# Moving the output projection behind the next block's last convolution, and the first weight loads behind the first transposes, in a two-layer hybrid encoder step

## The chip, the cores and the metric

The kernel runs on one core of one Trainium2 chip. The engines are named as in the profile: PE (TensorE matmul, with PEld for its weight loads), DVE (VectorE), ACT (ScalarE), POOL (GpSimd) and SP (SyncE, whose queue starts most DMA transfers). The metric is the device time of one execution in microseconds (us), as the median of several runs; less is better. "Span" is the time from the first to the last instruction of the profiled execution.

## The reference

One step of a streaming encoder with two layers. Layer A is a gated recurrent block; layer B is sliding-window attention over keys and values that are computed once from layer A's result. There are two groups of rows: a prompt of 4096 rows and a "sample" group of 8 x 16 = 128 rows with a saved state. The model width is 1024. Layer A, cut to what matters here:

```python
def a_layer(x, conv_hist, h0, norm_g, w_in, conv_w, conv_b, wa, ba, wx, bx, lam, w_out):
    u = rms_norm(x, norm_g) @ w_in
    xb, gate = u[..., :D_RNN], u[..., D_RNN:]
    xc, conv_new = causal_conv(xb, conv_hist, conv_w, conv_b)    # width 4
    h, h_last = rglru(xc, h0, wa, ba, wx, bx, lam)
    y = (h * jax.nn.silu(gate)) @ w_out
    return x + y, conv_new, h_last

def rglru(x, h0, wa, ba, wx, bx, lam):
    ...
    r = jax.nn.sigmoid(gr)      # gr, gi: two products of x with 256 x 256 gate blocks
    i = jax.nn.sigmoid(gi)
    log_a = RG_C * r * jax.nn.log_sigmoid(lam.astype(jnp.float32))
    a = jnp.exp(log_a)
    b = jnp.sqrt(-jnp.expm1(2.0 * log_a)) * (i * xf)
    ...
    _, h = lax.associative_scan(comb, (a, b), axis=1)
```

Layer B (queries, windowed softmax with sinks, a second gated projection) isn't touched by the change, except for three transfers that it starts early.

## The kernel before

**Precision.** Every matrix product is made of three float16 products: an operand is split into a high and a low part (`hi`, `lo`), and `mm3` (L221) issues hi x hi, hi x lo, lo x hi for each of the 8 slices of the contraction. So a product over 1024 channels is 24 matmuls. Weights are split at the start of the kernel: `Prep` (L105) loads a weight tile, takes the largest absolute value of each of its slices (`largest`, L126: L132 on ACT, L134 on DVE), gets one scale from them through a tiny PE product (`inv_scale`, L94), and `finish` (L153) writes `hi` (L172, L175) and `lo` (L173, L176) into the same tile. The activations before the output projection are split in the same way, with a scale taken from their own largest value (`BlockA.split`, L543).

**Blocks.** The prompt is 16 blocks of 256 rows. For layer A a block does four pairs p of 256 channels. `conv(p)` is 48 matmuls for the left half of `w_in`, then ACT copies the result (`U`, L462), POOL and DVE make the four taps (`xc`, L474 and L476) and `xchl` holds the split of it (L478, L479). `silu(p)` is 48 matmuls for the right half and gives `v` (L487, L488). `gates(p)` (L491) is 24 matmuls for r and i from `xchl`, then a chain on ACT (`tr`, `ti`, `th`, `a`) and DVE (`ti`, the scan L526) that gives `hg` and its largest value `amax` (L539). When all four pairs are there, `split` makes the scale (PE, then DVE `m2h` to `ish`) and then `hghl`: four `hi` on ACT (L554), four `lo` on DVE (L555). `out(u)` (L561), for u = 0 to 3, is 24 matmuls of `hghl` with `w_out` (128 rows x 512 columns), adds the input rows `xr` again (L572), stores the sum, and after the last of them `norm_out` (L581) computes the row norm and writes the rows, split, to the DRAM buffer `xq` for layer B. A block's own input comes from `load` (rows `xt`), `rstd` (squares, L415), `norm` (L418: `xp` as hi on ACT, lo on DVE, L213 and L214) and four DMA transposes into `xn` (L426).

**Order.** PE's instructions run in the order in which they are written. From the third block on (i = 2 to 15; i = 1 has its own branch) one turn of the loop in `layer_a` (L605) gives PE this: conv(0), silu(0), gates(3) of the block before, conv(1), silu(1), gates(0), conv(2), silu(2) with the scale of the block before in its middle, gates(1), the four out(u) of the block before, conv(3), silu(3), gates(2). In the last turn (i = 15) one out(u) stands there, and the other three later. The other engines' queues are ordered when the program is built, by a simulated timeline; what each then runs is fixed. `after(e, i)` puts the instructions of a `with` body behind instruction i in the queue of i's engine. `step()` hangs pieces of layer B's weight preparation (`bw`, `bp`) between these parts.

**Start.** The sample group `bs` is loaded first, then block 0 (`b0`). The loads of the first pairs' weights go through `e.wload`, which is ACT's queue for pair 0, the first gates and pair 1, and SP's queue afterwards; nothing ties a load to the transposes, so the builder's order decides. `w0` to `w3` are the four pairs' weight tiles, `w5` and `w6` hold raw slices for them.

Of the kernel before, what the change touches and what calls it, by code (L numbers as in the profile page):

```python
# [10 lines left out]
F32 = mybir.dt.float32  # L11
# [8 lines left out]
P = 128  # L20
# [83 lines left out]
class Prep:  # L104
# [6 lines left out]
    def __init__(self, e, w, src, ranges, ends, pool, act=()):  # L111
        nc = e.nc
        self.act = act
        self.e, self.w, self.ranges, self.pool = e, w, ranges, pool
        pieces, wid = w.shape[1:]
        n_in = pieces - 2
        self.raw = [w[:, k + 2] for k in range(n_in)]
        for h in range(0, n_in, 3):
            g = min(h + 3, n_in)
            e.wload(w[:, h + 2:g + 2], src[:, h:g])  # L120
        self.src = src[:, n_in:]
        self.mx = e.sm.tile([P, len(ranges)], F32, name=f"mx{len(ranges)}", bufs=2 if len(ranges) < 8 else 3)
        self.largest(range(n_in))
        if ends is not None:
            self.rest(ends)
# [11 lines left out]
    def rest(self, ends):  # L137

        if isinstance(ends, list):
            for k, t in enumerate(ends):  # L140
                self.e.wload(t, self.src[:, k])
        else:
            self.e.wload(ends, self.src)
            ends = [ends[:, k] for k in range(2)]
        n = len(self.raw)
        self.raw += ends
        self.largest((n, n + 1))
        return self
# [115 lines left out]
def a_weights_head(e):  # L264

    nc = e.nc
    v = e.vec
    work = e.tmp.tile([P, 2, NB], F32, name="tr", bufs=1).rearrange("p a b -> p (a b)")
    t, z, z2, acc = (work[:, KT * i:KT * i + KT] for i in range(4))
    lam = v[:, V_LAM]  # L270
    nc.scalar.activation(t, lam, AF.Abs)
    nc.scalar.activation(t, t, AF.Exp, scale=-1.0)
    nc.vector.tensor_scalar(z, t, 2.0, None, op0=OP.add)
    nc.vector.reciprocal(z, z)
    nc.vector.tensor_tensor(z, z, t, op=OP.mult)
    nc.vector.tensor_tensor(z2, z, z, op=OP.mult)
    nc.vector.tensor_scalar(acc, z2, 1.0 / 21, 1.0 / 19, op0=OP.mult, op1=OP.add)
    for d in (17, 15, 13, 11, 9, 7, 5, 3, 1):
        nc.vector.tensor_tensor(acc, acc, z2, op=OP.mult)
        nc.vector.tensor_scalar(acc, acc, 1.0 / d, None, op0=OP.add)  # L280
    nc.vector.tensor_tensor(acc, acc, z, op=OP.mult)
    nc.vector.tensor_scalar(t, lam, 0.0, None, op0=OP.min)
    nc.vector.scalar_tensor_tensor(t, acc, -2.0, t, op0=OP.mult, op1=OP.add)
    e.clh = e.keep.tile([P, KT], F32, name="clh")
    e.nclh = e.keep.tile([P, KT], F32, name="nclh")
    nc.vector.tensor_scalar(e.clh, t, 4.0, None, op0=OP.mult)
    nc.vector.tensor_scalar(e.nclh, t, -4.0, None, op0=OP.mult)
# [104 lines left out]
class BlockA:  # L392
# [25 lines left out]
    def norm(self):  # L418
# [3 lines left out]
        for st, x in enumerate(self.x):  # L422
            hi, lo = self.xp[st], e.tmp.tile([P, 1024], F16, name="xp", bufs=3)
            pair_rows(e, x, self.r[:, st:st + 1], hi, lo)
            for a, t in enumerate((hi, lo)):
                nc.sync.dma_start_transpose(out=self.xn[:, a, :, st * P:(st + 1) * P], in_=t)  # L426
        self.mx = e.sm.tile([P, 4], F32, name="amax")

    def proj(self, p, half, mid=None):
# [130 lines left out]
    def out(self, u, each=False):  # L560
# [7 lines left out]
        W = e.wO[o]  # L568
        run(mm3(e, ps, lambda k, a: h[:, a, k, st * P:(st + 1) * P], lambda k, b: part(W, k, b, 0, 512), range(KT)))
        x = e.tmp.tile([P, 512], F32, name=e.t_res, bufs=e.b_res)  # L570
        e.load(x, self.src[st, :, 512 * o:512 * o + 512])
        dve = nc.vector.scalar_tensor_tensor(x, ps, self.inv[:, o:o + 1], x, op0=OP.mult, op1=OP.add)  # L572
        e.anchor = dve, e.anchor[1]
        e.store(e.x1[self.bi][st, :, 512 * o:512 * o + 512], x)
# [31 lines left out]
def layer_a(e):  # L606
# [2 lines left out]
    blocks = [BlockA(e, i) for i in range(e.nblk)]  # L609
    b0 = blocks[0]  # L610
    bs.load()
    e.wload = lambda o, i: e.nc.scalar.dma_start(o, i)
    bs.rstd()
    bs.norm()
    b0.load()
    a_weights_head(e)
    a_pair_load(e, 0)
    a_pair_gload(e, 0)
    a_pair_load(e, 1)
    e.wload = e.load  # L620
    a_pair_in(e, 0)
    b0.rstd()
    b0.norm()
    a_pair_gload(e, 1)
    a_pair_gin(e, 0)
    for p in range(4):
        bs.conv(p)
# [11 lines left out]

        b0.conv(p, mid)  # L640
        if p < 3:
            with after(e, e.prep[p + 1][0].ready):
                if p < 2:
                    a_pair_load(e, p + 2)
                    a_pair_gload(e, p + 2)
# [8 lines left out]
        bs.gates(p)  # L654
    e.store(e.outs["s_conv"], e.sconv)
    e.store(e.outs["s_h"], e.sh0)
    a_out_load(e)
    prev = b0
    wb = b_weights(e)
    for i in range(1, e.nblk):  # L660
# [51 lines left out]
        if first:  # L712
# [8 lines left out]
            b.gates(2)  # L721
            cache_load(e)
        else:
            for o in range(1 if last else 4):
                prev.out(o, last)
                step()
            b.conv(3, step)
            step()
            if last:
                e.store(e.outs["p_conv"], e.hist)  # L730
            b.silu(3)
# [136 lines left out]
def b_consts(e):  # L868
# [13 lines left out]

    qk, e.qsc, e.nsf, e.bias = k([P, 2, 64]), k([P, 18]), k([P, 8]), k([P, 192])
    e.nsink, e.nsfs, e.bias_s, e.nsink_s = k([P, 8]), k([P, 2]), k([P, 2, 144]), k([P, 2])
    e.load(store[:, 0:used[0]], e.ins["b_consts"])
    e.gk = qk[:, 1]
    f = k([P, 64])
    nc.vector.scalar_tensor_tensor(f, qk[:, 0], 0.125, qk[:, 1], op0=OP.mult, op1=OP.mult)
# [365 lines left out]


def layer_b(e, prev, tail):
    e.store(e.outs["s_old"], e.ins["cache_tail"])
    e.cc0 = e.tmp.tile([P, 2, 2, 384], F16, name="cc0", bufs=1)
    bs = BlockB(e, -1)
    bs.xn = e.xs  # L1260
# [86 lines left out]
def tile_kernel(ctx, tc, ins, outs):  # L1347
# [8 lines left out]
    e.big = pool("big", 1)  # L1356
    e.dram = pool("dram", 1, space=DRAM)
    e.load = lambda o, i: nc.sync.dma_start(o, i)
    e.wload = e.load
    e.store = lambda o, i: nc.sync.dma_start(o, i)  # L1360
    e.cols = e.keep.tile([P, 96], F32, name="cols")
    e.one8 = e.keep.tile([P, KT], F32, name="one8")
# [111 lines left out]
```

## Time and profile before

| | |
|---|---|
| median of 3 runs | 2738.92 us (2738.11 to 2741.18) |
| the profiled execution | 2738.68 us, of which its span is 2736.3 us |
| busy in the span | PE 2568.0, DVE 1941.0, ACT 1631.3, POOL 510.9 us |
| DMA | 295.80 MB in 538494 packets |
| PE's granted clock, mean | 0.976 |

The page of the profile gives busy time by engine, then 40 slices of the span with one digit per slice (tenths busy; for PEclk the granted clock in tenths). The timeline lists instructions in order of time, equal neighbours merged: start, duration, engine, line, operation, tiles, count, and in brackets the idle time before it and what ended that. The table of windows gives, for each stretch: its length, each engine's busy time (and instructions), the granted clock, the DMA share and GB/s. The table of waits gives who waited for whom: us in total, times, longest. The chain of waits follows the work that ended last back from the end.

### The profile page before, as it was taken

The numbers are of one execution on the slowest core, as the hardware profiler recorded it, in microseconds if no ns is written. First come the engines' busy times: TensorE is split into PE (matmuls) and PEld (weight loads), VectorE is DVE, ScalarE is ACT, GpSimd is POOL, SyncE is SP. The second block draws the span as 40 slices with busy tenths as digits, with TensorE's granted clock in tenths as the row PEclk, the third lists the DMA queues.
The fourth block names the chain that finished last, engine by engine and source line by source line (L and its number), as shares of the span: only waits on it lengthen the run. The fifth ranks groups of instructions, "written<-read, shape, count | busy, mean of one in ns | idle before, by whom it ended". The sixth has DMA issues, their size and how long they took to land.

```text
span 2736.3 us, 51574 instructions
## 1 busy us (share of the span) xinstructions
PE 2568.0 (94%) x18838; PEld 1773.6 (65%) x18838; DVE 1941.0 (71%) x6101; ACT 1631.3 (60%) x3784; POOL 510.9 (19%) x624
## 2 busy tenths in 40 slices
PE   3788999999999999999998999999999999999998
PEld 2675677666677766667756656666665566666654
DVE  5977776667676676767666867777777677777675
ACT  4765675565676756567645655555555555555554
POOL 1432111111111111111112211111222111112220
PEclk9889999999999999999999999999999999999999
DMA  7032333333232433333555555454544554545444
GB/s 267 9 103 71 90 77 111 101 107 110 83 109 88 147 101 108 109 89 100 197 145 155 107 114 109 109 108 95 100 91 105 112 109 110 108 96 102 90 89 97
DMA packets 538494, 295.80 MB, mean 108 GB/s; under 512 B 454384, under 2 KB 467696, under 8 KB 536688
## 3 DMA queue, kind: packets, MB, share of 16 engines
q1 hardware_dynamic: 537232, 287.80, 42.1%
q10 hardware_dynamic: 1008, 4.72, 0.4%
q8 instruction: 147, 2.41, 0.4%
q14 instruction: 107, 0.88, 0.1%
HBM read 112.05 MB, written 66.86 MB: 65 GB/s over the span
## 4 chain that ended last, share of the span: by engine, by line
PE 56%; DVE 16%; ACT 13%; DMA 6%; issue 6%; POOL 2%; SPq 0%; ACTq 0%; DVEq 0%; POOLq 0%
PE pm L229 51%; DVE xc L476 4%; PE pa L1099 3%; PE po L1144 3%; DMA xn<-xp 2%; DVE ti L526 2%; ACT a L510 1%; ACT th L509 1%; ACT ti L508 1%; DMA xq<-xp 1%; POOL xc L474 1%; ACT L513 1%; DVE hg L538 1%; ACT tr L507 1%; DVE ti L515 1%
## 5 line engine op out<-in xcount | busy, mean ns | idle before, releaser
L229 PEld LDWEIGHTS <-w 128*128 128x128 f16 x9792 | 943.5, 99 | 161.8 <-issue 26.2
L229 PE MATMUL pm<-xn,w 128*128 128x256 f16 (+1 forms) x8064 | 900.3, 273 | 44.0 <-DMA xn<-xp 29.9
L229 PE MATMUL pm<-w,hghl 128*128 128x512 f16 x3120 | 729.0, 389 | 57.3 <-ACT hghl L554 52.0
L229 PEld LDWEIGHTS <-hghl 128*128 128x128 f16 x3120 | 303.8, 100 | 430.4 <-ACT hghl L554 56.4
L1107 ACT ACTIVATE s<-s,negm 128x192 f32<-128x192 f32 (+2 forms) x512 | 226.5, 443 | 194.9 <-DVE negm L1104 193.3
L1122 DVE SCALAR_TENSOR_TENSOR ph<-s,ri,ph 128x64 f16<-128x64 f32 x1008 | 247.4, 314 | 46.0 <-ACT ph L1118 45.8
L229 PEld LDWEIGHTS <-w4b 128*128 128x128 f16 x1968 | 190.6, 99 | 114.0 <-issue 9.9
L1104 DVE CUSTOM_DVE_ANT_0 s<-pa,cst 128x192 f32<-128x192 f32 (+2 forms) x512 | 223.0, 470 | 45.0 <-PE pa L1099 42.9
L1118 ACT ACTIVATE ph<-s,ri 128x192 f16<-128x192 f32 (+2 forms) x512 | 191.0, 440 | 87.2 <-ACT d L1249 54.8
L476 DVE SCALAR_TENSOR_TENSOR xc<-U,cws,xc 128x256 f32<-128x256 f32 (+1 forms) x408 | 181.2, 477 | 18.0 <-POOL xc L474 17.8
L1156 POOL TENSOR_TENSOR hghl<-hg,hghl 128x512 f16<-128x512 f32 (+1 forms) x65 | 75.4, 1170 | 617.5 <-DVE xt L1238 523.9
L229 PE MATMUL pm<-w,xn 128*128 128x512 f16 x816 | 183.3, 381 | 5.4 <-DVE xn L555 3.5
L229 PEld LDWEIGHTS <-xn 128*128 128x128 f16 x1200 | 116.5, 98 | 103.0 <-issue 4.7
L229 PE MATMUL pm<-w4b,w 128*128 128x256 f16 x1536 | 176.9, 273 | 0.0
L229 PE MATMUL pm<-w,w4b 128*128 128x512 f16 x768 | 172.9, 381 | 0.0
L465 POOL COPY hist<-U 128x6 f32<-128x6 f32 x60 | 16.9, 281 | 633.6 <-ACT U L462 633.6
L474 POOL TENSOR_SCALAR xc<-U,cws,cbs 128x256 f32<-128x256 f32 (+1 forms) x136 | 114.7, 850 | 77.5 <-DVE ti L514 23.8
L1099 PE MATMUL pa<-kT,qT 128*128 128x192 f16 (+2 forms) x1024 | 125.1, 245 | 4.0 <-ACT qT L1061 4.0
L1099 PEld LDWEIGHTS <-qT 128*128 128x128 f16 x1024 | 91.5, 98 | 40.7 <-ACT qT L1061 5.3
L1048 POOL TENSOR_TENSOR qh<-qf,qh 128x512 f16<-128x512 f32 x66 | 77.8, 1198 | 185.4 <-ACT qh L1047 185.4
L220 ACT ACTIVATE junk<-xr 128x512 bf16<-128x512 f32 x60 | 37.5, 624 | 124.9 <-DVE xr L572 120.1
L229 PE MATMUL pg<-xchl,w4b 128*128 128x256 f16 (+1 forms) x816 | 95.8, 274 | 12.3 <-POOL w4b L176 7.1
(286 smaller groups left out, 3559.2 us busy)
## 6 DMA issues: line engine op xcount, KB each, us to landing
xt<-in_xp_dram SPq DMA_DIRECT2D x32, 512.0 KB, 4.4
xt<-x SPq DMA_DIRECT2D x64, 256.0 KB, 2.7
out_yp_dram<-xt SPq DMA_DIRECT2D x64, 256.0 KB, 2.3
xr<-in_xp_dram SPq DMA_DIRECT2D x58, 256.0 KB, 4.6
x<-xr SPq DMA_DIRECT2D x58, 256.0 KB, 2.1
xq<-xp SPq DMA_DIRECT2D x58, 256.0 KB, 3.5
bw<-in_b_q_dram SPq DMA_DIRECT2D x32, 256.0 KB, 3.4
bw<-in_b_gate_dram SPq DMA_DIRECT2D x32, 256.0 KB, 3.1
```

The source lines that it names most:

```text
L229: nc.tensor.matmul(ps, w(k, a), x(k, b), start=(i == 0 and j == 0), stop=(i == len(ks) - 1 and j == 2))
L474: nc.gpsimd.tensor_scalar(o, tap(t, 0), e.cws[:, 0, j:j + 1], e.cbs[:, 0, j:j + 1], op0=OP.mult, op1=OP.add)
L476: dve = nc.vector.scalar_tensor_tensor(o, tap(t, k), e.cws[:, k, j:j + 1], o, op0=OP.mult, op1=OP.add)
L526: nc.vector.tensor_tensor_scan(h[:, t], a[:, t], ti[:, t], 0.0 if self.sample else e.carry[:, j:j + 1], op0=OP.mult, op1=OP.add)
L1048: nc.gpsimd.tensor_tensor(qh[:, :, 1], qf, qh[:, :, 0], op=OP.subtract)
L1099: nc.tensor.matmul(ps[:, y, lo:192], qT[:, j2 + y, c], self.kT[:, 2 * g + x, k0 + lo:k0 + 192], start=x == 0, stop=x == 1)
L1104: nc.vector.tensor_tensor_reduce(s_[:, y, lo:192], ps[:, y, lo:192], e.bias[:, lo:], scale=e.nsf[:, h:h + 1], scalar=e.nsink[:, h:h + 1], ...
L1107: nc.scalar.activation(s_[:, y, lo:192], s_[:, y, lo:192], AF.Exp, bias=negm[:, j:j + 1], scale=-1.0, accum_out=den[:, j:j + 1])
L1118: nc.scalar.activation(hi[:, lo:], ss[j][:, lo:192], AF.Copy, scale=ri[:, j:j + 1])
L1122: nc.vector.scalar_tensor_tensor(ph[:, j, to:to + n], ss[j][:, cols], ri[:, j:j + 1], hi[:, cols], op0=OP.mult, op1=OP.subtract)
L1144: nc.tensor.matmul(po[64 * g:64 * g + 64, :], V[:, 64 * g:64 * g + 64], PT[g][:, :, b, :], start=i == 0, stop=i == len(prods) - 1)
L1156: nc.gpsimd.tensor_tensor(self.hl[:, 1][sl], og, hi, op=OP.subtract)
```

## The change

Two things are moved, and nothing is added to the arithmetic. First, in the loop of layer A, for i = 2 to 14 the four out(u) of the block before, and for i = 15 the one out(u), stand behind conv(3) of the running block and ahead of its silu(3). Second, the start of layer A is put in another order: all weight loads go through SP's queue; the sample group's `rstd` and `norm` get high priority for the builder; pair 0's weights are loaded ahead of block 0's rows; the gates' weights and pair 1 are put behind the sample group's transposes (`turned`, the last of them), pairs 2 and 3 behind block 0's; and the residual rows `xr`, the output weights, layer B's constants and the copy of the old cache stay behind block 0's transposes too.

```diff
-            e.wload(w[:, h + 2:g + 2], src[:, h:g])
+            e.load(w[:, h + 2:g + 2], src[:, h:g])
...
             for a, t in enumerate((hi, lo)):
-                nc.sync.dma_start_transpose(out=self.xn[:, a, :, st * P:(st + 1) * P], in_=t)
+                self.turned = nc.sync.dma_start_transpose(out=self.xn[:, a, :, st * P:(st + 1) * P], in_=t)
...
         x = e.tmp.tile([P, 512], F32, name=e.t_res, bufs=e.b_res)
-        e.load(x, self.src[st, :, 512 * o:512 * o + 512])
+        with after(e, e.turned):
+            e.load(x, self.src[st, :, 512 * o:512 * o + 512])
...
     bs.load()
-    e.wload = lambda o, i: e.nc.scalar.dma_start(o, i)
-    bs.rstd()
-    bs.norm()
...
+    with e.tc.high_priority():
+        bs.rstd()
+        bs.norm()
+    a_pair_load(e, 0)
     b0.load()
     a_weights_head(e)
-    a_pair_load(e, 0)
-    a_pair_gload(e, 0)
-    a_pair_load(e, 1)
-    e.wload = e.load
     a_pair_in(e, 0)
     b0.rstd()
     b0.norm()
-    a_pair_gload(e, 1)
+    with after(e, bs.turned):
+        a_pair_gload(e, 0)
+        a_pair_load(e, 1)
+        a_pair_gload(e, 1)
     a_pair_gin(e, 0)
...
         b0.conv(p, mid)
         if p < 3:
-            with after(e, e.prep[p + 1][0].ready):
+            with after(e, e.prep[p + 1][0].ready), after(e, b0.turned):
...
     e.store(e.outs["s_h"], e.sh0)
-    a_out_load(e)
+    e.turned = b0.turned
+    with after(e, e.turned):
+        a_out_load(e)
...
         else:
+            b.conv(3, step)
+            step()
             for o in range(1 if last else 4):
                 prev.out(o, last)
                 step()
-            b.conv(3, step)
-            step()
```

**SP's queue at the start**, from the sample group's rows `xt` on. Before (`xn<-xp` are the transposes; `w` are weight tiles; rows of the same transfers that follow each other are merged):

```order
L1358 DMA xt<-in_xs_dram 128x1024
L1358 DMA xt<-in_xp_dram 128x1024
L298 DMA sstate<-in_state_conv_dram 128x192
L301 DMA sstate<-in_state_rglru_dram 128x64
L1358 DMA w_218<-in_a_gates_dram 128x1024
L1358 DMA w_624<-in_a_w_in_dram 128x1536 x2
L1358 DMA w_219<-in_a_w_in_dram 128x1024
L1358 DMA w_218<-in_a_gates_dram 128x1024
L1358 DMA w_1022<-in_a_w_in_dram 128x1536 x2
```

Six more transfers follow there (weights, `hghl`, two of `xr`), and then the sample group's two transposes, the 19th and the 21st transfer of the queue. The same place now, from the same transfer on:

```order
L1363 DMA xt<-in_xs_dram 128x1024
L1363 DMA w_164<-in_a_w_in_dram 128x1536 x2
L1363 DMA w_136<-in_a_w_in_dram 128x1024
L1363 DMA xt<-in_xp_dram 128x1024
L296 DMA sstate<-in_state_conv_dram 128x192
L299 DMA sstate<-in_state_rglru_dram 128x64
L421 DMA_TRANSPOSE xn<-xp 128x8x128 x2
L1363 DMA xt<-in_xp_dram 128x1024
L1363 DMA w_135<-in_a_gates_dram 128x1024
L1363 DMA w_335<-in_a_w_in_dram 128x1536 x2
L1363 DMA w_136<-in_a_w_in_dram 128x1024
L1363 DMA w_135<-in_a_gates_dram 128x1024
```

Pair 0's weights (`w_164`, `w_136`) came to this queue from ACT's; the two transposes of the sample group moved ahead of pair 1 (`w_335`), which came from ACT's queue too. Block 0's four transposes stand right behind these rows, ahead of pairs 2 and 3.

**DVE at the start**, in the second half of the split of pair 0's weights (`w_220`, now `w_164`; `mx_250`, now `mx_338`, are the largest values of pair 1's weights, `w_247`, now `w_335`; `w_219`, now `w_136`, holds raw slices of both). Before:

```order
L134 TENSOR_REDUCE mx_250<-w_247 128x1 x3
L173 SCALAR_TENSOR_TENSOR w_220<-w_220,gs_262 128x512
L362 TENSOR_SCALAR sstate<-sstate,cols 128x48
L350 TENSOR_TENSOR pairw<-pairw,acw 128x2
L173 SCALAR_TENSOR_TENSOR w_220<-w_220,gs_262 128x512
L351 TENSOR_TENSOR pairw<-pairw,vabs 128x2
L134 TENSOR_REDUCE mx_250<-w_219 128x1 x2
L173 SCALAR_TENSOR_TENSOR w_220<-w_220,gs_262 128x512
```

Three more low parts (L173) follow there, and block 0's row norm behind them. Now, as far as the last low part and the reductions of pair 1's gates (`mx_350`):

```order
L134 TENSOR_REDUCE mx_338<-w_335 128x1 x3
L173 SCALAR_TENSOR_TENSOR w_164<-w_164,gs_239 128x512
L205 TENSOR_TENSOR rtn_301<-ryn_300 128x2
L173 SCALAR_TENSOR_TENSOR w_164<-w_136,gs_239,w_164 128x512
L134 TENSOR_REDUCE mx_338<-w_335 128x1 x3
L134 TENSOR_REDUCE mx_338<-w_136 128x1 x2
L206 TENSOR_TENSOR rtn_301<-rtn_301,rxn_299 128x2
L173 SCALAR_TENSOR_TENSOR w_164<-w_136,gs_239,w_164 128x512
L134 TENSOR_REDUCE mx_350<-w_135 128x1 x2
```

The last low part of pair 0 stands behind all eight reductions of pair 1 now (before, four low parts stood behind them), and the arithmetic of block 0's norm (`rtn_301`) runs through the list and ends behind it.

**ACT around the out(u)**, from the last `junk` (the squares of `xr`) of a block on, seventh turn. Before:

```order
L220 ACTIVATE junk,ss_8382<-xr 128x512 x2
L213 ACTIVATE xp<-xr,rb 128x512 x3
L462 ACTIVATE U<-pm 128x2x256
L213 ACTIVATE xp<-xr,rb 128x512
L415 ACTIVATE xp,ss_8889<-xt 128x1024 x2
L487 ACT_TABLE_LOAD
L487 ACTIVATE v<-pm,cols 128x512
L478 ACTIVATE xchl<-xc 128x512
L816 ACTIVATE bp<-bw,gs_8084 128x512
L507 ACTIVATE tr<-pg,hb,cols 128x256 x2
```

And now:

```order
L220 ACTIVATE junk,ss_8453<-xr 128x512 x2
L213 ACTIVATE xp<-xr,rb 128x512 x3
L482 ACT_TABLE_LOAD
L482 ACTIVATE v<-pm,cols 128x512
L502 ACTIVATE tr<-pg,hb,cols 128x256 x2
L504 ACTIVATE th<-tr,nclh 128x256
L505 ACTIVATE a<-tr,clh 128x256
L213 ACTIVATE xp<-xr,rb 128x512
```

`U` and `xchl` of conv(3) left this place (they stand ahead of the `junk` now), and the squares of the next rows (`xp,ss`) moved behind the first gate activations (`tr`, `th`, `a` of gates(2)).

More of the change, by code (lines that the diff above doesn't have):

```diff
@@ L140, in rest @@
             for k, t in enumerate(ends):
-                self.e.wload(t, self.src[:, k])
+                self.e.load(t, self.src[:, k])
         else:
-            self.e.wload(ends, self.src)
+            self.e.load(ends, self.src)
             ends = [ends[:, k] for k in range(2)]
@@ L289, in a_weights_head @@
     nc.vector.tensor_scalar(e.hb, v[:, V_BA:V_BX + 1], 0.5, None, op0=OP.mult)
-    e.vabs = e.keep.tile([P, 12, KT], F32, name="vabs")
-    nc.scalar.activation(e.vabs, v, AF.Abs)
     e.acw = e.keep.tile([P, KT], F32, name="acw")
@@ L611, in layer_a @@
     bs.load()
-    e.wload = lambda o, i: e.nc.scalar.dma_start(o, i)
-    bs.rstd()
-    bs.norm()
+    e.vabs = e.keep.tile([P, 12, KT], F32, name="vabs")
+    e.nc.scalar.activation(e.vabs, e.vec, AF.Abs)
+    e.gW = [e.wp.tile([P, 2, 2, 512], F32, name=f"w4{h}") for h in "ab"]
+    e.raw_g, e.raw_in = (e.wp.tile([P, KT, 512], F32, name=f"w{i}") for i in (5, 6))
+    e.wA, e.useff, e.sgate, e.sga, e.prep = [], [], [], [], {}
+    with e.tc.high_priority():
+        bs.rstd()
+        bs.norm()
+    a_pair_load(e, 0)
     b0.load()
     a_weights_head(e)
-    a_pair_load(e, 0)
-    a_pair_gload(e, 0)
-    a_pair_load(e, 1)
-    e.wload = e.load
     a_pair_in(e, 0)
@@ L884, in b_consts @@
     e.nsink, e.nsfs, e.bias_s, e.nsink_s = k([P, 8]), k([P, 2]), k([P, 2, 144]), k([P, 2])
-    e.load(store[:, 0:used[0]], e.ins["b_consts"])
+    with after(e, e.turned):
+        e.load(store[:, 0:used[0]], e.ins["b_consts"])
     e.gk = qk[:, 1]
@@ L1256, in layer_b @@
 def layer_b(e, prev, tail):
-    e.store(e.outs["s_old"], e.ins["cache_tail"])
+    with after(e, e.turned):
+        e.store(e.outs["s_old"], e.ins["cache_tail"])
     e.cc0 = e.tmp.tile([P, 2, 2, 384], F16, name="cc0", bufs=1)
@@ L1358, in tile_kernel @@
     e.load = lambda o, i: nc.sync.dma_start(o, i)
-    e.wload = e.load
     e.store = lambda o, i: nc.sync.dma_start(o, i)
```

3 lines of the change are left out of this document (removed).

## The prediction

> **What bounds the kernel now.** I read the page first, for which engine is the bound and where it isn't busy.
>
> ```profile
> span 2736.3 us, 51574 instructions
> PE 2568.0 (94%) x18838; PEld 1773.6 (65%) x18838; DVE 1941.0 (71%) x6101; ACT 1631.3 (60%) x3784; POOL 510.9 (19%) x624
> ```
>
> PE is busy for 94% of the span, so the kernel is bound by PE nearly everywhere, and what can be won is PE's idle time and the time in which its clock isn't full. To see where both lie I cut the span into its stages with the table of windows: the start (up to the first turn's end), the loop of layer A from i = 2 on, the passage to layer B, and layer B.
>
> ```profile
> 0.00:312.00 312.00, 225.17 (x1930) 182.40 (x1931) 233.27 (x693) 194.83 (x358) 91.06 (x122) 0.91 0.37 114
> 312.00:1367.00 1055.00, 996.75 (x7586) 747.20 (x7585) 734.95 (x1682) 680.70 (x1133) 174.05 (x261) 0.97 0.36 107
> 1367.00:1500.00 133.00, 119.98 (x947) 76.64 (x945) 82.13 (x288) 69.31 (x176) 21.59 (x22) 0.97 0.57 157
> 1500.00:2736.30 1236.30, 1226.07 (x8382) 767.38 (x8380) 890.68 (x3441) 686.45 (x2119) 224.22 (x219) 1.00 0.49 102
> ```
>
> The first number after the stretch is its length, the next PE's busy time; the clock stands third from the end. PE idles 86.8 us in the start, 58.3 in the loop, 13.0 in the passage and 10.2 in layer B, and the clock is below full in the first three. The change touches the first two. In the loop the table of waits for PE has these two rows (and a third of 3.6 us, once):
>
> ```profile
> PE pm L229 <- ACT hghl L554: 50.6, 14, 5.2
> PE pm L229 <- DVE hghl L555: 3.2, 7, 0.6
> ```
>
> So nearly all of it is one place, met once in each of 14 turns: PE has finished gates(1) and waits for the split `hghl` of the block before, which out(0) needs. One turn, from PE's timeline:
>
> ```profile
> 717.80 2.78 PE L229 MATMUL pg<-xchl,w4a 128*128 128x256 f16 x24
> 725.34 23.67 PE L229 MATMUL pm<-w,hghl 128*128 128x512 f16 x96 [4.76 <-ACT hghl L554]
> 748.85 10.64 PE L229 MATMUL pm<-xn,w 128*128 128x256 f16 x96
> ```
>
> The third row is conv(3) with silu(3), which wait for nothing that the split makes. They are what the change puts (its first half) into the gap.
>
> **Loop: what the gap costs.** The wait isn't all of it. The same matmuls, in the 14 turns together and in the first turn (i = 1), where they follow others without a gap:
>
> ```profile
> 312.00:1367.00 1055.00, 304.58 (x1272) 0.97 0.36 107
> 250.50:272.00 21.50, 20.88 (x96) 1.00 0.43 124
> ```
>
> At the first turn's rate 1272 of them take 1272 / 96 x 20.88 = 276.7 us; they took 304.6. The 27.9 us between are slow clock behind the gap, as a window of one turn shows it:
>
> ```profile
> 486.00:488.00 2.00, 2.00 (x6) 0.74 (x5) 1.97 (x4) 1.97 (x3) 0.00 (x0) 0.50 0.00 0
> 484.22 0.60 PE L229 MATMUL pm<-w,hghl 128*128 128x512 f16 x2 [3.00 <-ACT hghl L554]
> ```
>
> The clock is 0.50 there, after a gap of only 3.00. So the place costs 50.6 + 3.2 + 27.9 = **81.7 us**, 5.8 a turn.
>
> [...]
>
> **Loop: what is left of it.** Moving conv(3) doesn't lengthen or shorten PE's work between one block's last out(u) and the next block's first: before it was conv(3), silu(3), gates(2) ... gates(1), now it is silu(3), gates(2) ... gates(1), conv(3). The gap exists because the chain on ACT and DVE that ends in the split takes longer than that. The next turn, PE's rows first and then rows of the chain of waits from the last out(u), which ended at 748.85:
>
> ```profile
> 798.85 2.78 PE L229 MATMUL pg<-xchl,w4a 128*128 128x256 f16 x24
> 804.90 0.61 PE L229 MATMUL pm<-w,hghl 128*128 128x512 f16 x2 [3.26 <-ACT hghl L554]
> 753.01 0.73 ACT xp L213
> 759.02 0.61 ACT xp L415
> 760.08 1.14 ACT xp L415 x2
> 761.23 1.28 ACT L487
> 762.52 0.69 ACT v L487
> 764.34 0.91 ACT tr L507 x2
> ```
>
> Counted from 748.85, PE's work is done after 52.8 (798.85 + 2.78) and the first `hghl` is there after 56.0: the wait of 3.26. Gates(2) gets its first activation (`tr`) after 15.5. What stands in these 15.5? Norm and split of the output rows (`xp` from 4.2), conv(3)'s `U` and `xchl`, the squares of the next rows (L415, which waited for stores of `xq`), and PE itself, which needs 10.64 for conv(3) and silu(3) and 2.78 for gates(2), so 13.4.
>
> Now PE ends gates(2) after half of the 10.64 and 2.78, 8.1, and in ACT's new order `U`, `xchl` and the squares no longer stand ahead. ACT's path is 4.2 to the first `xp`, three of 0.73, the table load 1.28 and `v` 0.69: 8.4. So `tr` starts after 8.4 and not 15.5, **7.1 earlier**. Against that the squares (0.61 + 1.14 and their waits, say 2.5) come back behind `tr`. If all of them lengthen the rest of the chain, `hghl` is ready after 56.0 - 7.1 + 2.5 = 51.4; if they fall into ACT's waits for PE, after 48.9. PE asks for it at 52.8. The gap of this turn closes with 1.4 to 3.9 us over; the turn with the longest wait (5.2, so 1.9 more) comes out between 0.5 late and 2 early. Some low parts will be late as now (3.2 us in all). I leave 4 of the 81.7: **minus 78 us**, with nothing left and 43 left (a rival, below) as ends.
>
> What conv(3) itself costs in its new place: its six taps are 6 x 0.477 on DVE, during the out(u).
>
> ```profile
> L476 DVE SCALAR_TENSOR_TENSOR xc<-U,cws,xc 128x256 f32<-128x256 f32 (+1 forms) x408 | 181.2, 477 | 18.0 <-POOL xc L474 17.8
> 725.30:748.80 23.50, 23.31 (x96) 9.78 (x97) 15.01 (x24) 14.75 (x26) 0.62 (x1) 0.89 0.40 124
> ```
>
> DVE is busy for 15.0 of the 23.5 us there and ACT for 14.8; 2.9 and some 1.2 more fit. In the shared accumulators (`pm`, five buffers) conv(3) takes the one of silu(0), long read, and the last out(u) takes that of silu(2), some us after `v` has read it. So I cost this at nothing; the cover is the 8.5 us that DVE has free.
>
> **Start.** PE's first rows, and what they wait for:
>
> ```profile
> PE pm L229 <- DMA xn<-xp: 29.9, 4, 20.3
> 15.24 1.28 DVE L214 SCALAR_TENSOR_TENSOR xp<-xt,r,xp 128x1024 f16<-128x1024 f32 x1
> 28.52 4.83 SPq L426 DMA_TRANSPOSE xn<-xp  x1
> 34.07 2.65 SPq L426 DMA_TRANSPOSE xn<-xp  x1
> 30.37 0.75 DVE L173 SCALAR_TENSOR_TENSOR w<-w,gs,w 128x512 f16<-128x512 f32 x1
> 39.43 7.91 PE L229 MATMUL pm<-xn,w 128*128 128x128 f16 x95 [1.42 <-DMA xn<-xp]
> 46.77 0.15 DVE L207 SCALAR_TENSOR_TENSOR r<-rtn,ryn 128x2 f32<-128x2 f32 x1
> 55.89 4.45 PE L229 MATMUL pm<-xn,w 128*128 128x256 f16 x20 [2.72 <-DMA xn<-xp]
> ```
>
> The sample rows are split at 16.5, but their first transpose leaves SP at 28.5, behind the weights of three later pairs. PE starts at 39.4, block 0 follows at 55.9. With the transposes ahead of pair 1 they leave at 15 to 17, and PE's start is then set by the last low part of pair 0's weights. In DVE's new order the same number of low parts and reductions stands ahead of it, so 31.1 as before if data are there. Pair 1's loads leave later now, at about 18 if a transpose costs SP what block 0's do (four in 5.86, 1.3 each with short waits), or up to 5 later if the 4.83 and 2.65 above aren't the full queue's doing; 3 MB at the 365 GB/s of the first 25 us are 8.2. That gives 26 to 31 for the last reduction's data, where DVE was at 26: I take 2 late, **33**, with 31 and 37 as ends. Block 0's norm ends behind it: two reductions of 0.37, some 0.5, seven steps of 0.2, so 35.6 instead of 46.9. From there to PE's start it was 55.9 - 46.9 = 9.0; block 0 begins at 44.6, 11 us earlier.
>
> ```profile
> 48.13 5.86 SPq L426 DMA_TRANSPOSE xn<-xp  x4
> 0.00:25.00 25.00, 0.79 (x2) 0.60 (x3) 17.83 (x84) 13.29 (x32) 0.70 (x6) 1.00 0.94 365
> 100.00:125.00 25.00, 19.91 (x234) 17.75 (x233) 23.38 (x77) 20.78 (x38) 10.39 (x14) 1.00 0.01 2
> ```
>
> What follows is bound by the preparation of pairs 1 to 3 (in 100 to 125 DVE is busy for 23.4 of 25 us), and it moves along. Two us of it I take off: layer B's constants, which DVE computed while it was idle, now stand in this stretch. **Minus 9 us**; 0 if that preparation sets the pace regardless, 13 at most. Pair 0's loads leave ACT's queue for SP's, right behind the sample rows; that is three issues of 0.3 to 0.5 on SP, and the sample rows have the DMA engines to themselves at first: nothing, 2 us to each side. Loads of pairs 2 and 3 behind block 0's transposes cost nothing: they leave by 46, and their slices are first read tens of us later.
>
> **Sum.** 2738.7 (the profiled execution, 0.2 under the median) - 78 - 9 = **2652 us**. Layer B's orders are the same from its second block on.
>
> **Rivals.** *The squares and the fourth `xp` hold ACT* (half the gain). That `xp` and the squares wait for stores of `xq`, and now stand amid gates(2). In one turn a store took 5.3 us:
>
> ```profile
> 674.13 5.32 DMA xq<-xp
> 1425.91 2.84 PE L229 MATMUL pm<-xs,w 128*128 128x128 f16 x48
> 1435.86 0.22 PE L1183 MATMUL pa<-cc,qT 128*128 128x128 f16 x1 [1.93 <-ACT cc L1169]
> 1436.92 4.46 PE L229 MATMUL pm<-xs,w 128*128 128x128 f16 x48
> ```
>
> If this costs the chain 4 us more, a gap of about 1.5 stays, and slow clock with it: at 1436.9, behind a gap of 1.93, 48 matmuls took 4.46 that took 2.84 at 1425.9. 14 x (1.5 + 1.6) = 43 left: 2691. For it: the chain already ran through such stores. Against: they leave earlier relative to `tr` now.
>
> *The start wins nothing*: pair 1's data come at 31 and later, or the preparation sets the pace: 2661.
>
> *Slower: conv(3) makes DVE late for the last `xr`*. Its taps stand in order ahead of the out(u)'s rows; if they wait for POOL or a buffer until after the last out(u), norm and chain start late by L, each turn. The gap is then L - 1.4 with 2.0 of slow clock, and from L = 5.2 on a turn costs more than its 5.8 now. At L = 9 it is 7.6 + 2.0, 3.8 a turn more: 53 more, 9 less, 2783. Beyond its 2.9 the taps would have to hold DVE for the 5.6 that are left free and 9 more; no row shows such a wait.
>
> *The change does nothing in the loop*, as the chain keeps its 56.0: 2730. The new order of ACT speaks against it.
>
> **How the numbers follow.** Forecast 0.65 (by itself 2640 to 2661), no gain at the start 0.14, half the loop 0.14, nothing in the loop 0.03, slower 0.04. The range 2636 to 2692 holds the first three with the ends of the unknown costs. About 0.2% (5.5 us) is what a measurement here can tell from no change: faster 0.94, same 0.02, slower 0.04.
>
> **What would show it.** In the new profile: no row of PE waiting for `hghl` over 1 us in the loop; the turn at about 74 us instead of 79.5; out(u) of 96 matmuls in 20.9; clock 1.00 between the start and 1300; `tr` of gates(2) 8 to 9 us behind the last out(u); sample transposes at 15 to 17, block 0's first product at about 45. It would be wrong if the gap only moves: to silu(3), to gates(2), or to the next block's rows.

## The result, and the profile after

The changed kernel takes **2671.53 us** (median of 4 runs, 2670.49 to 2672.72); the kernel before takes 2739.94 in the runs beside it. The ratio is 0.9751, with a 95% interval of 0.9734 to 0.9768. The forecast was 2652, in a range of 2636 to 2692. Of the 87 us that it took off, 66 came: the profiled execution took 2672.72, that of before 2738.68.

The page's first lines, and then the table of windows for the loop (after the stretch: its length, PE's busy time; the clock stands third from the end):

```profile
span 2670.9 us, 51579 instructions
PE 2550.5 (95%) x18838; PEld 1775.8 (66%) x18838; DVE 1929.3 (72%) x6101; ACT 1628.8 (61%) x3784; POOL 504.9 (19%) x624
```

```profile
303.00:1291.00 988.00, 967.11 (x7547) 743.34 (x7545) 711.24 (x1662) 669.39 (x1115) 165.83 (x259) 0.99 0.38 111
```

PE idled 58.3 us in the loop before and idles 20.9 now; the clock rose from 0.97 to 0.99 and isn't full (1.00 was forecast). What PE waits for, from the table of its waits (total, times, longest):

```profile
PE pss L88 <- DVE m1h L80: 14.5, 5, 4.5
PE pss L88 <- DVE m2c L90: 5.3, 1, 5.3
PE pm L229 <- DVE hghl L550: 0.2, 1, 0.2
```

The row of ACT's `hghl` is gone, and DVE's 0.2 is all that is left of it. But there is a row that before didn't have: the scale matmul in the middle of silu(2) waits for `m1h`, the largest value of the previous block's `hg`, from which the split takes its scale. Five times: in every second turn. Two turns from PE's timeline, an undisturbed one and the next:

```profile
612.62 20.88 PE L229 MATMUL pm<-w,hghl 128*128 128x512 f16 x96
633.34 5.40 PE L229 MATMUL pm<-xn,w 128*128 128x256 f16 x48
675.49 0.39 PE L88 MATMUL pss<-ident,m1h 128*128 128x128 f32 x2
675.71 2.78 PE L229 MATMUL pm<-xn,w 128*128 128x256 f16 x24
...
686.19 20.88 PE L229 MATMUL pm<-w,hghl 128*128 128x512 f16 x96
706.91 5.40 PE L229 MATMUL pm<-xn,w 128*128 128x256 f16 x48
752.35 0.79 PE L88 MATMUL pss<-ident,m1h 128*128 128x128 f32 x2 [3.36 <-DVE m1h L80]
752.94 5.29 PE L229 MATMUL pm<-xn,w 128*128 128x256 f16 x24
765.93 4.26 PE L229 MATMUL pm<-w,hghl 128*128 128x512 f16 x19
```

From out(u) to out(u) the first turn takes 73.57, the second 79.74: 3.36 of it is the wait, and behind it the same 24 matmuls take 5.29 instead of 2.78. The five such turns take 75.5, 79.7, 80.5, 77.4 and 76.2, together 21.5 us more than five of 73.56. That is as much as the forecast missed. The gap ahead of the out(u) was closed, and it opened again some 10 us earlier in PE's order (675.49 and 686.19 in the undisturbed turn).

Why every second turn? ACT's rows from the timeline, first those of the kernel before behind gates(1) of one turn, then those of the changed kernel in the disturbed turn above (`bp` is a piece of layer B's split weights, `junk<-xr` the square of a finished row, the three `xp` the first output rows after the norm):

```profile
733.34 0.72 ACT L816 ACTIVATE bp<-bw,gs 128x512 f16<-128x512 f32 x1
738.30 0.72 ACT L816 ACTIVATE bp<-bw,gs 128x512 f16<-128x512 f32 x1 [1.69 <-DMA q<-bp]
742.93 0.72 ACT L816 ACTIVATE bp<-bw,gs 128x512 f16<-128x512 f32 x1 [1.08 <-DMA q<-bp]
746.94 0.72 ACT L816 ACTIVATE bp<-bw,gs 128x512 f16<-128x512 f32 x1 [3.28 <-DMA q<-bp]
753.01 1.95 ACT L213 ACTIVATE xp<-xr,rb 128x512 f16<-128x512 f32 x3 [2.40 <-DVE rb L207]
```

```profile
692.54 0.73 ACT L819 ACTIVATE bp<-bw,gs 128x512 f16<-128x512 f32 x1
696.72 0.72 ACT L819 ACTIVATE bp<-bw,gs 128x512 f16<-128x512 f32 x1 [1.03 <-DMA q<-bp]
704.35 0.72 ACT L819 ACTIVATE bp<-bw,gs 128x512 f16<-128x512 f32 x1 [0.62 <-DMA q<-bp]
708.34 0.72 ACT L819 ACTIVATE bp<-bw,gs 128x512 f16<-128x512 f32 x1 [1.00 <-ACT junk L220]
712.56 0.72 ACT L819 ACTIVATE bp<-bw,gs 128x512 f16<-128x512 f32 x1 [3.50 <-DMA q<-bp]
713.19 0.61 ACT L220 ACTIVATE junk<-xr 128x512 bf16<-128x512 f32 x1
717.04 1.95 ACT L213 ACTIVATE xp<-xr,rb 128x512 f16<-128x512 f32 x3 [2.39 <-DVE rb L207]
720.89 1.01 ACT L502 ACTIVATE tr<-pg,hb,cols 128x256 f32<-128x256 f32 x2
```

Before, four pieces stood ahead of the last row's square, now five. All go through one buffer (`bp`, bufs=1), so a piece waits until the store of the piece before has landed, about 4.1 us from piece to piece. The fifth comes at 712.56, 5.65 us after the last out(u) has ended (706.91), and the squares of the last two rows stand behind it in ACT's order. So the first `xp` comes 10.1 us behind the last out(u) (4.2 before, and 4.2 now in the undisturbed turns), `tr` of gates(2) 14.0 behind it, and `m1h` follows. Layer B's weights are prepared in groups: one turn takes the maxima, the next splits the pieces; hence every second turn. A sixth turn has pieces too, that of i = 3: its first `xp` comes 8.6 behind, and there it is the cache's second scale matmul that waits, for `m2c` (5.3, and 3.6 before), ahead of the next `m1h`. This was the theory (**A**) that went into the experiments; its rivals stand with them.

### The profile page after: what moved, and what is told of

It is laid out like the page before. It is cut to its first block, busy times and chain, and to the rows that moved or that the text cites. A ratio compares the mean times of both kernels' runs of the same rounds, so it can differ in the third digit from the quotient of the medians.

```text
span 2670.9 us, 51579 instructions
## 1 busy us (share of the span) xinstructions
PE 2550.5 (95%) x18838; PEld 1775.8 (66%) x18838; DVE 1929.3 (72%) x6101; ACT 1628.8 (61%) x3784; POOL 504.9 (19%) x624
## 3 DMA queue, kind: packets, MB, share of 16 engines
q1 hardware_dynamic: 538240, 292.52, 44.6%
## 4 chain that ended last, share of the span: by engine, by line
PE 61%; DVE 13%; ACT 11%; DMA 7%; issue 5%; POOL 2%; SPq 0%; ACTq 0%; DVEq 0%; POOLq 0%
PE pm L229 54%; PE pa L1103 3%; DVE xc L471 3%; PE po L1148 3%; PE pg L229 2%; DMA xn<-xp 2%; DVE ti L521 1%; ACT xp L213 1%; DVE hg L533 1%; ACT a L505 1%; ACT ti L503 1%; ACT L508 1%; ACT th L504 1%; ACT bp L819 1%; DVE bp L820 1%
## 5 line engine op out<-in xcount | busy, mean ns | idle before, releaser
L229 PE MATMUL pm<-xn,w 128*128 128x256 f16 (+1 forms) x8064 | 910.3, 274 | 34.8 <-DVE w L173 17.0
L229 PE MATMUL pm<-w,hghl 128*128 128x512 f16 x3120 | 702.4, 380 | 1.3 <-POOL hghl L1160 1.1
L1126 DVE SCALAR_TENSOR_TENSOR ph<-s,ri,ph 128x64 f16<-128x64 f32 x1008 | 247.0, 312 | 44.6 <-ACT ph L1122 44.2
L469 POOL TENSOR_SCALAR xc<-U,cws,cbs 128x256 f32<-128x256 f32 (+1 forms) x136 | 105.8, 786 | 97.4 <-ACT U L457 42.0
L1018 POOL TENSOR_TENSOR sq<-qf 128x512 f32<-128x512 f32 x66 | 69.1, 1048 | 176.4 <-ACT qf L1016 150.1
```

The costliest lines, as they stand in the source:

```text
L229: nc.tensor.matmul(ps, w(k, a), x(k, b), start=(i == 0 and j == 0), stop=(i == len(ks) - 1 and j == 2))
L469: nc.gpsimd.tensor_scalar(o, tap(t, 0), e.cws[:, 0, j:j + 1], e.cbs[:, 0, j:j + 1], op0=OP.mult, op1=OP.add)
L1018: nc.gpsimd.tensor_tensor(sq, qf, qf, op=OP.mult)
L1126: nc.vector.scalar_tensor_tensor(ph[:, j, to:to + n], ss[j][:, cols], ri[:, j:j + 1], hi[:, cols], op0=OP.mult, op1=OP.subtract)
```

## The experiments

**The two parts apart.** The start alone is the changed kernel with the loop's order of before, as this diff has it; the loop alone is the kernel before with the reverse of it:

```
-            b.conv(3, step)
-            step()
             for o in range(1 if last else 4):
                 prev.out(o, last)
                 step()
+            b.conv(3, step)
+            step()
```

> Everything of the change but the loop's order: conv(3) stands behind the out(u) again. Theory (the start's gain is carried through unshortened to the end): the first turn's out(u) begins at 240 to 242 as in the changed kernel (before 250.9), PE waits for hghl 50 us in the loop as before, time 2739.9 - 10 = 2730 (2727 to 2733). Rival (the start's gain is only an earlier beginning and a later stage waits it away, as the transfers of the rows or of layer B's weights don't move): 2737 to 2740.

> Only the loop's order: conv(3) ahead of the out(u), with the start of before. Theory (both parts are independent and add up to 68): first out(u) at 251, hghl waits gone, waits for m1h in every second turn as in the changed kernel, 2739.9 - 58 = 2682 (2678 to 2686). Rival (the waits for m1h come from the start's new order, which shifts the layer B pieces against the turns): no waits for m1h, all turns at 73.6, 2662 or less.

The start alone: 2725.64, ratio 0.9951 (0.9938 to 0.9963), so 13 us; the loop alone: 2688.77, ratio 0.9816 (0.9803 to 0.9830), so 50. Together 64 of the 67 to 68 that both give at once. In the one, PE waits for `hghl` as before; in the other, for `m1h` as in the changed kernel:

```profile
PE pm L229 <- ACT hghl L549: 53.7, 15, 4.7
```

```profile
PE pss L88 <- DVE m1h L80: 17.5, 5, 4.9
```

Both parts carry through to the end, and the waits for `m1h` belong to the loop's new order, not to the start. Both sizes were missed by a few us (2730 and 2682 expected). Of the start's 13 us, 10.6 are there by the first out(u) (240.31); where the rest comes from isn't shown.

**A second buffer for the pieces.**

```
-        w = e.tmp.tile([P, 512], F32, name="bp", bufs=1)[:, :wid]
+        w = e.tmp.tile([P, 512], F32, name="bp", bufs=2)[:, :wid]
```

> The changed kernel with two buffers instead of one for bp, the pieces of layer B's split weights that pass through ACT and DVE between the out(u). Theory A (in every second turn the pieces go through one buffer, each waits about 4 us for the store of the piece before, and ACT, which works in order, gets to the squares of the last rows of x 6 us late; norm, gates(2), gates(3) and m1h follow 6 us late): no wait of PE for m1h over 0.5 us from 500 us on, the first xp 4 to 5 us behind the last out(u) in all turns (10.1 in the disturbed one), those five turns at 73.6 instead of 75.5 to 80.5, 2671.5 - 21 = 2651 (2647 to 2656). Rival B (m1h is late because conv(3)'s taps, the squares of the next block's rows and the fourth xp stand in the chain of every turn): waits for m1h stay, 2668 to 2673.

2653.73, ratio 0.9686 (0.9673 to 0.9699). The waits for `m1h` fell from 14.5 to 2.4 us, and the five turns to between 73.4 and 75.5; the first `xp` comes 6.0 to 7.6 behind the last out(u) there. That isn't the 4 to 5 that I expected: a second buffer helps, but the load of the next piece (`bw`) is then waited for. ACT's row in the turn whose wait stayed longest, 1.85:

```profile
700.28 0.72 ACT L819 ACTIVATE bp<-bw,gs 128x512 f16<-128x512 f32 x1 [5.70 <-DMA bw<-in_b_q_dram]
```

Rival B (conv(3)'s taps, the squares and the fourth `xp`, which are in the chain of every turn) is out: none of these was touched.

**The same buffer in the kernel before.** Is the second buffer worth its 18 us by itself?

> The kernel before with two buffers for bp and nothing else. Theory A (the pieces of bp were late there too, but the first xp came 4.2 us behind the last out(u) in both kinds of turns, so they weren't what ended last; conv(3)'s move made them so): the hghl waits stay at 45 to 55 us, time 2735 to 2740. Rival C (two buffers help by themselves, whatever conv(3)'s place: the 18 us that they won in the changed kernel are theirs alone): 2718 to 2725.

2741.01, ratio 1.0014 (1.0006 to 1.0023): nothing won. The first `xp` comes 4.2 behind the last out(u) there in every turn, with one buffer or two. So one buffer for the pieces cost nothing until conv(3) was moved.

**The scale four steps earlier.** An attempt to move the pieces away from the out(u):

```
             b.silu(0)
-            step()
+            step(True)
...
             b.silu(1)
-            step(True)
+            step()
```

> The changed kernel with one buffer for bp, but the scale of layer B's weights is made available four steps earlier in the turn (after silu(0) instead of silu(1)), so that the pieces start one gate stage earlier and fewer stand among the out(u). Theory A: the last piece among the out(u) comes before the last rows, the first xp 4 to 6 us behind the last out(u), waits for m1h under 5 us in all (14.5 now), 2651 to 2662. Rival B (as above): 2668 to 2673 with the waits for m1h unchanged.

2699.71, ratio 0.9854 (0.9839 to 0.9869), slower than the changed kernel by 28 us, against both theories' numbers. The edit didn't do what I meant: ACT's order puts five pieces ahead of the last row's square here too, and they come later than in the changed kernel. In the turn whose last out(u) ends at 715.81:

```profile
720.83 0.72 ACT L819 ACTIVATE bp<-bw,gs 128x512 f16<-128x512 f32 x1 [2.75 <-DMA q<-bp]
724.48 0.72 ACT L819 ACTIVATE bp<-bw,gs 128x512 f16<-128x512 f32 x1 [0.66 <-DMA q<-bp]
728.26 1.95 ACT L213 ACTIVATE xp<-xr,rb 128x512 f16<-128x512 f32 x3 [2.45 <-DVE rb L207]
```

```profile
PE pss L88 <- DVE m1h L80: 19.9, 5, 4.9
```

The first `xp` comes 12.5 behind the last out(u), the waits for `m1h` grow to 19.9, and the one wait in the turn i = 3, 5.3 in the changed kernel, to 7.1. So the run makes the same lateness larger instead of curing it; why the pieces come later isn't known, and the run doesn't tell the theories apart as it was meant to.

**conv(3)'s two steps behind silu(3).** If conv(3) took its two steps of layer B's weights along, and with them the fifth piece, then putting these two back behind silu(3) must undo it, with one buffer:

```
-            b.conv(3, step)
-            step()
+            b.conv(3)
             for o in range(1 if last else 4):
                 prev.out(o, last)
                 step()
...
             b.silu(3)
             step()
+            step()
+            step()
```

> The changed kernel with one buffer for bp, but the two steps of layer B's weights that went along with conv(3) (one in its middle, one behind it) follow silu(3) instead. In ACT's order four pieces of bp then stand amid the out(u), as in the kernel before, and the fifth behind v. Theory A (conv(3) took its two steps along, and with them a fifth piece came among the out(u); five pieces at 4.1 us each don't fit into the out(u)'s 20.9): first xp 4 to 5.5 us behind the last out(u) in all turns, waits for m1h under 3 us in all (14.5 in the changed kernel), 2650 to 2658. Rival D (the pieces are late whatever their number, since the scale for them comes late in the turn): first xp still 8 to 10 late, 2668 to 2673.

**2645.84**, ratio 0.9656 (0.9643 to 0.9670): 26 us under the changed kernel, and more than I expected. The turn that corresponds to the one above (last out(u) ended at 699.69), on ACT, and the one wait of PE in the middle of the loop:

```profile
697.20 0.72 ACT L820 ACTIVATE bp<-bw,gs 128x512 f16<-128x512 f32 x1 [0.61 <-DMA q<-bp]
...
701.24 0.72 ACT L820 ACTIVATE bp<-bw,gs 128x512 f16<-128x512 f32 x1 [2.71 <-DMA q<-bp]
...
705.72 1.95 ACT L213 ACTIVATE xp<-xr,rb 128x512 f16<-128x512 f32 x3 [2.39 <-DVE rb L207]
...
708.98 0.69 ACT L482 ACTIVATE v<-pm,cols 128x512 f32<-128x512 f32 x1
709.57 0.71 ACT L820 ACTIVATE bp<-bw,gs 128x512 f16<-128x512 f32 x1
```

```profile
PE pss L88 <- DVE m2c L90: 2.1, 1, 2.1
```

The row of `m1h` is gone. The fifth piece stands behind `v` (at 709.57), where its buffer is free and it costs 0.7 us of ACT. Rival D is out. Of the 26 us, 21.5 are the five turns and 4.7 the sixth, that of i = 3 (80.9 in the changed kernel, 76.2 here). The table below puts the runs side by side: how far the first `xp` is behind the last out(u) in the five turns with pieces, and how long PE then waits for `m1h` (from the timelines; an undisturbed turn has 4.2). Two of the five turns, with 5.6 and 6.0, still lie over the 5.5 that was expected of this run.

| kernel | first `xp` behind, us | wait for `m1h`, us |
|---|---|---|
| before | 4.2 4.2 4.3 4.2 4.2 | none |
| conv(3)'s steps behind silu(3) | 4.4 6.0 5.6 5.3 4.3 | none |
| two buffers | 6.0 7.6 6.4 6.4 6.0 | 0, 1.85, 0.36, 0.22, 0 |
| changed kernel | 8.6 10.1 9.7 9.0 8.2 | 1.86, 3.36, 4.49, 2.18, 2.63 |
| scale earlier | 12.4 12.5 14.5 13.7 10.7 | 3.37, 4.95, 4.61, 3.70, 3.29 |

In this table there is no wait up to 6.0, and one from 6.4 on. In the two runs below the border is less sharp: with everything together 6.3 and 6.2 went with 1.1 and 1.0; with the cache's matmuls in two turns another 6.3 went with none, and 5.8 with 1.0, in the turn that got the second of these matmuls. So the turn had room for roughly 2 us of lateness.

**The cache's two scale matmuls in two turns** (with two buffers), and **everything together** (with conv(3)'s steps behind silu(3) as well); the new argument picks one of the two:

```
-            if i == 3:
-                cache_max(e)
+            if i in (3, 5):
+                cache_max(e, i == 5)
```

> The kernel with two buffers for bp, and the two scale matmuls of the cache (at the end of the turn i = 3, the second waits 1.0 us there and 5.3 in the changed kernel for the first one's m2c on DVE) in two different turns, i = 3 and i = 5. Theory: no wait for m2c, the turn of i = 3 at 73.6 instead of 75.1, 2652 (2648 to 2655), within the measurement of the one with two buffers. Rival (the added matmul in i = 5 meets a busy DVE as well and holds up the shared one-buffer accumulator for m1h): a new wait of 2 to 5 us there, 2655 to 2660.

> The last one with two buffers for bp as well, and the cache's two scale matmuls in two turns. Theory: nothing waits in the loop but the last turns' flush of what is left of layer B's weights; all turns of i = 3 to 14 at 73.6 to 74.0, 2644 to 2650. If what is left in the kernel with two buffers isn't the pieces, 2649 as that one with the cache's matmuls apart.

2649.24, ratio 0.9680 (0.9667 to 0.9694), and 2648.16, ratio 0.9665 (0.9652 to 0.9679). The wait for `m2c` is gone in both, but waits for `m1h` stay, 3.1 us in four turns and 2.1 in two. The first run's rival is right in kind: a new wait stands in the turn i = 5, of 1.0 us and not 2 to 5. Neither run is told apart from conv(3)'s steps behind silu(3) alone, at 0.9656. That one has the lowest time and the smallest edit.

**The start: which waits for transposes count.** Three kernels leave out some of the change's waits: those of pair 1's weights for the sample rows' transposes; those of pairs 2 and 3 for block 0's; all of them, the rows' and the out weights' too.

```
-    with after(e, bs.turned):
-        a_pair_gload(e, 0)
-        a_pair_load(e, 1)
-        a_pair_gload(e, 1)
+    a_pair_gload(e, 0)
+    a_pair_load(e, 1)
+    a_pair_gload(e, 1)
```

```
-            with after(e, e.prep[p + 1][0].ready), after(e, b0.turned):
+            with after(e, e.prep[p + 1][0].ready):
```

```
-        with after(e, e.turned):
-            e.load(x, self.src[st, :, 512 * o:512 * o + 512])
+        e.load(x, self.src[st, :, 512 * o:512 * o + 512])
...
-    with after(e, e.turned):
-        a_out_load(e)
+    a_out_load(e)
```

The third has all three edits, and the last one also at layer B's constants and at the cache's tail.

> The changed kernel, but the loads of pair 1's weights and of the gates of pairs 0 and 1 don't wait for the sample rows' transposes: SP issues these six loads just ahead of the two transposes instead of just behind them. Theory S (what counts is that the transposes stand ahead of the weights): the transposes' data come after pair 1's 2.5 MB, the sample rows' first product at 22 to 26 instead of 15.7, block 0's at 47 to 51 instead of 43.5, time 2675 to 2680. Rival T (DVE's chain, which waits for pair 1's data before the last low part of pair 0, sets the pace): pair 1's data come earlier, block 0's product at 41 to 44, time 2668 to 2672.

> The changed kernel, but the loads of pairs 2 and 3 don't wait for block 0's transposes: SP issues them ahead of everything but pair 0, so also ahead of the sample rows' transposes and of pair 1. Theory S: as in the kernel before, the transposes' data come behind those of the weights, the first product of the sample rows after 28, block 0's at 52 to 58, time 2679 to 2684. Rival T: pair 1's data come 5 MB later too, so that this loses even if the transposes don't count; then the sample rows' first product stays under 20 and only the last low part of pair 0 and block 0 come late.

> The changed kernel without any of the change's waits for the transposes: the loads of all later pairs, the out weights, the residual rows, layer B's constants and the copy of the cache's tail go out as SP comes to them, so most of them ahead of the sample rows' or block 0's transposes. What stays of the start's change is its order, and pair 0's weights on SP's queue behind the sample rows instead of on ACT's. Theory S (the waits make the start's gain, above all those of pairs 2 and 3 and of the rows): the first out(u) at 247 to 251, time 2677 to 2682. Rival U (the order and the queue of pair 0 make it; the loads of pairs 2 and 3 ahead cost 3.5 of the 10, the rest nothing): first out(u) at 244 to 245, 2674 to 2678.

2673.46 (0.9768, 0.9754 to 0.9781), 2678.11 (0.9786, 0.9771 to 0.9800) and 2682.90 (0.9790, 0.9776 to 0.9803). PE's rows at the start, of the changed kernel and of the three:

```profile
15.74 0.29 PE L229 MATMUL pm<-xn,w 128*128 128x128 f16 x1 [1.78 <-ACT w L172]
30.75 5.99 PE L229 MATMUL pm<-xn,w 128*128 128x128 f16 x73 [3.20 <-DVE w L173]
43.46 4.93 PE L229 MATMUL pm<-xn,w 128*128 128x256 f16 x23 [3.46 <-DMA xn<-xp]
```

```profile
21.47 0.26 PE L229 MATMUL pm<-xn,w 128*128 128x128 f16 x1 [7.30 <-DMA xn<-xp]
28.61 6.12 PE L229 MATMUL pm<-xn,w 128*128 128x128 f16 x73 [0.73 <-DVE w L173]
41.17 5.09 PE L229 MATMUL pm<-xn,w 128*128 128x256 f16 x23 [3.29 <-DMA xn<-xp]
```

```profile
26.46 0.27 PE L229 MATMUL pm<-xn,w 128*128 128x128 f16 x1 [12.21 <-DMA xn<-xp]
49.77 5.09 PE L229 MATMUL pm<-xn,w 128*128 128x256 f16 x23 [4.55 <-DMA xn<-xp]
```

```profile
34.09 0.27 PE L229 MATMUL pm<-xn,w 128*128 128x128 f16 x1 [19.38 <-DMA xn<-xp]
53.73 5.09 PE L229 MATMUL pm<-xn,w 128*128 128x256 f16 x23 [4.36 <-DMA xn<-xp]
```

The first out(u) begins at 240.75 in the changed kernel and at 241.1, 244.2 and 248.3 in these; at 250.9 before.

- Pair 1's place is worth nothing: with its loads ahead, the sample rows come 6 us later, and DVE's last low part 2 us earlier, which is what PE really waits for (rival T, whose time, 2672 at most, was missed by 1.5). Block 0's product comes 2.3 earlier too, and by the first out(u) that is gone again.
- Without the waits of pairs 2 and 3, 3.5 us are lost. Here neither theory has it all: the sample rows' first product, at 26.46, lies between T's "under 20" and S's "after 28", and block 0's is at 49.77, ahead of S's 52.
- Without any of the waits, 7.5 of the 10 us are lost, so about 4 more when the rest goes as well: the waits of the rows, the out weights, pair 1, layer B's constants and the cache's tail, which weren't taken apart. That is what theory S said of the first out(u), 247 to 251; the time is 0.9 over its range and 11 us over the changed kernel's, as the turns with pieces also came out a little longer.
- The remaining 2.6 is the new order with pair 0 on SP's queue. These two weren't taken apart either.

## Why the prediction was right, and where it fell short

- **The gap before out(0)**: right. Its 53.8 us of waits are gone. So is the slow clock behind it: the matmuls of the out(u), 729.0 us in all before, take 702.4, so 26.6 less where 27.9 were forecast, and 96 of them take 20.88 as forecast.

```profile
L229 PE MATMUL pm<-w,hghl 128*128 128x512 f16 x3120 | 729.0, 389 | 57.3 <-ACT hghl L554 52.0 <-DVE hghl L555 3.4 <-POOL hghl L1156 1.1
```

```profile
L229 PE MATMUL pm<-w,hghl 128*128 128x512 f16 x3120 | 702.4, 380 | 1.3 <-POOL hghl L1160 1.1 <-DVE hghl L550 0.2
```

- **The turn**: 74 forecast, 73.57 where nothing disturbs it. `tr` of gates(2) comes 8.0 behind the last out(u) there; 8.4 forecast, 15.5 before. The squares that come back cost 2.1 us of ACT, and the fourth `xp` had no wait. The roughly 2 us of room that the table shows lie within the margin of 1.4 to 3.9, but that margin was worked out for `hghl` at out(0), and the room is that of `m1h` at silu(2).
- **The step that failed** is "ACT's path is 4.2 to the first `xp`" in the loop's part, together with "what conv(3) itself costs in its new place: its six taps ... So I cost this at nothing". I took the 4.2 from a turn of the kernel before, which even had pieces of `bp` in it, and moved conv(3) as taps alone. But conv(3) carries two `step()`s, and each second step is a piece that ACT and DVE split and a store on SP's queue. Moved ahead of the out(u), they made five pieces of four, and the last came 5.65 us after the out(u). The price is 21.5 us in the five turns (78 forecast for the loop, of which about 54 came between the out(u) of i = 2 and of i = 15: 1040.2 before, 986.7 now). The two steps behind silu(3) win 26.
- **A wait that the forecast left out.** "Moving conv(3) doesn't lengthen or shorten PE's work between one block's last out(u) and the next block's first" holds for out(0), but not for the scale matmul in silu(2). Conv(3) stood between the last out(u) and this matmul, and now it stands behind the matmul. So PE asks for `m1h` 42.2 behind the last out(u) (675.49 less 633.34), where before, in the turn whose last out(u) ended at 748.85, it asked 47.2 behind:

```profile
796.01 0.39 PE L88 MATMUL pss<-ident,m1h 128*128 128x128 f32 x2
```

  On DVE, `m1h` was ready 42.7 behind the last out(u) there (791.5); it is ready after 39.4 in the undisturbed turn now (672.7), and after 45.4 in the disturbed one (752.3). So 4.5 us of room became 2.8 although the chain got shorter, and by these numbers even the disturbed turn's `m1h` would have been in time for the old place (no run tries that).
- **The rival "half the loop"** (2691) had the kind of event right, ACT held by a store, and the place wrong: not the stores of `xq` for the fourth `xp`, but those of `bp`. The time fell between it and the forecast, so that the range held it is in part luck: its upper part was drawn for another event. The warning "it would be wrong if the gap only moves" named silu(3), gates(2) and the next block's rows; it moved to silu(2).
- **The wait for `m2c`**, 3.6 us once and not in the sum, grew to 5.3, and the turn with it takes 80.9. With the pieces out of the way it shrinks to 2.1.
- **The start**: 9 forecast, 10.2 by the first out(u). The last low part's matmuls begin at 30.75 (33 forecast), block 0's product at 43.46 (44.6 forecast). The transposes left sooner than I said, at 11.65 instead of 15 to 17, and that was worth nothing, as the first of the three kernels shows: DVE's low parts set PE's start, as the forecast's text had it. The 30.75 is just under the low end of the forecast's 31 to 37. That pairs 2 and 3 load later "at no cost" had a wrong reason: pair 2's slices aren't first read tens of us later, but ACT waits for them at 46.67 and 48.66 (4.1 and 1.3 us). What these waits cost PE isn't shown; on balance holding the loads back paid, by the 3.5 us of the second kernel.

## What to carry to other kernels

When a step of a pipeline is moved, move on paper all that is hooked to it, side work of another stage above all: count its instructions in each engine's order in the new place, and the round trip of each buffer that they go through. Read the trace of a turn with the side work and of one without, and ask for each how much lateness the next consumer forgives (here 2 us). A gap that closes shows at once what stood behind it; a smaller edit than the change itself (two calls) was then worth more than a third of it again.

## What was not expected of the hardware

How much slow clock followed a gap of PE didn't go by the gap's length alone. After the wait of 2.18 in the middle of silu(2), the 24 matmuls behind took 4.13; after one of 2.63, at the same place two turns on, 2.78, as in an undisturbed turn:

```profile
1058.51 0.80 PE L88 MATMUL pss<-ident,m1h 128*128 128x128 f32 x2 [2.18 <-DVE m1h L80]
1059.10 4.13 PE L229 MATMUL pm<-xn,w 128*128 128x256 f16 x24
...
1209.93 0.49 PE L88 MATMUL pss<-ident,m1h 128*128 128x128 f32 x2 [2.63 <-DVE m1h L80]
1210.25 2.78 PE L229 MATMUL pm<-xn,w 128*128 128x256 f16 x24
```

The granted clock was 0.50 from 1059 to 1061, behind the shorter wait, and 1.00 from 1210 to 1213, behind the longer. In the changed kernel and in four of the runs (the loop alone, two buffers, the scale earlier, everything together) the waits for `m1h` of up to 1.86 left the 24 matmuls behind them at 2.78, and all from 2.92 on slowed them, to between 4.07 and 5.33. Only the two waits above lie between, and they went both ways.

What decides which of the two follows, no run shows. In the out(u), the forecast's clock term by the rows (27.9) came within 1.3 us of the measured 26.6.
